# Two of five gate tiles added element by element with indirect DMAs, the other three by reworked one-hot products, in a decoder-trunk step

## The chip, the cores and the metric

The kernel runs as one launch on 1 core of a Trainium2 chip. The metric is the device time of one execution in microseconds (us). PE is TensorE, DVE is VectorE, ACT is ScalarE, POOL is GpSimd, and SP is the queue that issues the plain DMAs.

## The reference, cut to what matters

One step of a decoder layer for 1024 prompt tokens and 32 sample tokens, width 1024: attention and a gated recurrence, cross attention, then PEER, a layer of 16384 single-neuron experts. The change lies in PEER:

```python
def one_block(xc):
    q = (xc @ w_pq).reshape(blk, PEER_HEADS, PEER_QDIM)
    ...
    v1, i1 = lax.top_k(s1, PEER_TOPK)      # 16 of 128 first keys
    v2, i2 = lax.top_k(s2, PEER_TOPK)      # 16 of 128 second keys
    ...
    sc, ci = lax.top_k(cand, PEER_TOPK)    # 16 of the 256 pairs
    e = (jnp.take_along_axis(i1, ci // PEER_TOPK, axis=-1) * PEER_NKEYS
         + jnp.take_along_axis(i2, ci % PEER_TOPK, axis=-1))
    g = jax.nn.softmax(sc, axis=-1)
    u = peer_u[e]
    a = jax.nn.gelu(jnp.einsum('td,thkd->thk', xc, u))
    return jnp.einsum('thk,thkd->td', (g * a), peer_v[e])
```

Each token picks 8 x 16 = 128 experts, each with a gate g. The same expert may be picked by several heads of one token; its gates add up.

## The kernel before, in words

The tokens lie in nine tiles of 128 (tile 8 holds the 32 sample tokens), in three parts: tiles 0, 1, 2; then 3, 4, 8; then 5, 6, 7. Part by part each goes through `middle` (projections, attention, recurrence) and `tail` (cross attention, then `select`, which finds each token's experts and gates). Stages overlap: the middle of a part runs beside the tail of the part before (`run(W1, ...)`, `run(W2, ...)`), the last tail beside the late gates (`run(W3, ...)`). Which instruction comes when on each engine is set by a scheduler that plans with its own estimates of durations; on the chip each engine then works its list off in that order.

PEER is done in two ways. Tiles 0 to 4 (640 tokens) are dense: 128 iterations in `dense` run over all experts, 128 in each. An iteration loads a block of u and of v, makes the products `a` of the 640 tokens with u in two halves of 320 (48 matmuls), takes Gelu, multiplies by a 128 x 640 piece of the gate matrix (tile `gt`, from the DRAM tensor `gtall`), and multiplies with v. Tiles 5 to 8 are gathered: for each tile rows of u and then of v come by indirect DMA on POOL (line 1177, 832 in all, 512 KB each), and DVE makes the dot products (line 1184) and the weighted sums (line 1195). The gathers run beside the dense pass and begin before it.

The gate matrix of a dense tile is built in `gates(di)`. `select` leaves for each token its 128 first indices, second indices and gates, transposed, in `selD`. For every token a matrix with a 1 at (slot, first index), `hot[0]`, and one with the gate at (slot, second index), `hot[1]`, are multiplied on PE: the product over the slots is the token's 128 x 128 gates. In groups of four tokens: one DVE comparison of 512 elements for `hot[0]` (L1013); four DVE operations (L1018) for `hot[1]`, or, for two tokens of the four in tiles 2, 3 and 4, two ACT operations each (L1021, L1022); four matmuls (L1024), each into 128 neighbouring PSUM columns; a copy (L1027) that interleaves the tokens into staging tiles `sg`, `row`, `thi` or `tlo`; after 16 tokens a store to `gtall`. Tile 0, 1 and 2 are built beside part 2's middle, tiles 3 and 4 beside its tail.

POOL has little to do before the gathers: 25 small power operations (`rs_r`, L211) of the norms. The list of POOL is worked off in order, and so are SP's issues: one that waits holds all behind it.

Of the kernel before, what the change touches and what calls it, by code (L numbers as in the profile page):

```python
# [25 lines left out]
NG = sum(t in PARTS[0] for t in DENSE)  # L26
GT = 16
# [38 lines left out]
def _body(tc, nc, ctx, A, O):  # L66
# [22 lines left out]
    anchors = []  # L89

# [32 lines left out]
    DM_A, DM_X, SEL, BEX = misc[:, 0:8], misc[:, 8:12], misc[:, 12:28], misc[0:32, 28:36]  # L123
    iota16 = T(cst, [128, 16], BF16, "iota16")
# [174 lines left out]
    def part(pi):  # L299
# [624 lines left out]
    def select_tile(t, R, H, v, ix, scale):  # L924
# [47 lines left out]
        if t in DENSE:  # L972
            p = bank(SELB)
            for i in range(3):
                PE.transpose(out=p[:, i * 128 : (i + 1) * 128], in_=fnd[:, i], identity=ident)
            st = T(pk, [128, 4, 128], F32, "c2", 2)
            pv = p[:, :384].rearrange("p (i t) -> p i t", i=3)
            S.copy(st[:, 0:3], pv)
            S.activation(st[:, 3], pv[:, 2], AF.Copy, scale=-1.0)
            SP.dma_start(selD[DENSE.index(t)], st)  # L980
            return
        eu = T(pk, [128, 128], U32, "sc")[:R, :n]
        V.scalar_tensor_tensor(eu, fnd[:, 0], 128.0, fnd[:, 1], op0=ALU.mult, op1=ALU.add)
# [9 lines left out]
    def gates(di):  # L993
        st = T(wk, [128, 4, 128], F32, "x_vs")
        SP.dma_start(st, selD[di])
        late_ = di >= NG
        for blk in range(128 // GT):
# [10 lines left out]
            w = 128 // len(stg)  # L1008
            for q in range(GT // 4):
                p = bank(("g", "Ty", "Ts")[flip("gb", LB)] if late_ else "g")  # L1010
                t0 = blk * GT + 4 * q
                hot = [T(wk, [128, 4, 128], F32, "raw" if RAW else "oh", 2 if RAW else 3), T(wk, [128, 4, 128], F32, "oh", 3)]
                V.tensor_tensor(hot[0], iota.rearrange("p (o k) -> p o k", o=1).to_broadcast([128, 4, 128]),  # L1013
                                st[:, 0, t0 : t0 + 4].rearrange("p (t o) -> p t o", o=1)
                                .to_broadcast([128, 4, 128]), op=ALU.is_equal)
                for i in range(4):
                    if i >= LATE[di]:
                        V.tensor_scalar(hot[1][:, i], iota, col(st[:, 1], t0 + i), col(st[:, 2], t0 + i),  # L1018
                                        op0=ALU.is_equal, op1=ALU.mult)
                    else:  # L1020
                        S.activation(hot[1][:, i], iota, AF.Abs, bias=col(st[:, 1], t0 + i), scale=-1.0)  # L1021
                        S.activation(hot[1][:, i], hot[1][:, i], AF.Relu, bias=col(st[:, 2], t0 + i),  # L1022
                                     scale=col(st[:, 3], t0 + i))
                    PE.matmul(p[:, i * 128 : (i + 1) * 128], lhsT=hot[0][:, i], rhs=hot[1][:, i],  # L1024
                              start=True, stop=True)
                for i, sg in enumerate(stg):
                    ANY.tensor_copy(sg[:, :, 4 * q : 4 * q + 4].rearrange("p i t -> p t i"),  # L1027
                                    p.rearrange("p (t i) -> p t i", i=128)[:, :, i * w : (i + 1) * w])
            for i, sg in enumerate(stg):
                SP.dma_start(gtd[di * (128 // GT) + blk][:, i * w : (i + 1) * w], sg)  # L1030
            if blk % 2:
                yield

    def dense(dv, dn, dps):
# [14 lines left out]
        NH = M // GT // 2  # L1049

        def gate_piece(k, h, r):
            lo, hi = max(0, 8 * k - 4 * h), min(128, 8 * k - 4 * h + 8)
            if lo >= hi:
                return
            if r == 0:
                gts[k, h] = T(dn, [128, NH, 8, GT], F32, "gt", 3)
            n = NH // 4
            ins = SP.dma_start(gts[k, h][:, r * n : (r + 1) * n, : hi - lo].rearrange("p b i t -> p b (i t)"),
                         gtall[h * NH + r * n : h * NH + (r + 1) * n, :, lo * GT : hi * GT].rearrange("b p x -> p b x"))
            if k == 0:  # L1060
                after(ins, GA[0] - GA[1] * (4 * (1 - h) + r))

        def hidden(i, out):
            if i == 0:
                for h in (1, 0):
                    for r in range(4):
                        gate_piece(0, h, r)
            k, h = divmod(i // 4 + 2, 2)
            gate_piece(k, 1 - h, i % 4)
# [6 lines left out]
            for h in range(2):  # L1076
                lo, hi = h * (M // 2), (h + 1) * (M // 2)
                kg, ki = divmod(i + 4 * h, 8)
                ki -= 4 * h if kg == 0 else 0
                pa = T(dps, [128, 512], F32, "a", 6 - 2 * KEEP + 1 if KEEP > 2 else 2)[:, : M // 2]  # L1080
                mm3(pa, u, x, 8, slice(lo, hi))
                S.activation(ga[:, lo:hi], pa, AF.Gelu)  # L1082
                gv = ga[:, lo:hi].rearrange("p (b t) -> p b t", t=GT)
                V.tensor_tensor(gv, gv, gts[kg, h][:, :, ki], op=ALU.mult)  # L1084
# [155 lines left out]
    run(W0, p[0].middle(lambda: ahead(p[1])), memory_kv())  # L1240
# [123 lines left out]
```

## Time and profile before

| | |
|---|---|
| time, median of 3 runs | 3661.61 us (3661.39 to 3673.91) |
| the profiled execution: time, span | 3667.75 us, 3665.9 us |
| mean granted TensorE clock | 0.968 |
| busy share PE / DVE / ACT / POOL | 93% / 71% / 38% / 31% |
| mean DMA rate | 275 GB/s |

The profiled execution was 6.1 us longer than the median of the runs. Busy shares are means over stages: POOL is idle in the first two fifths of the span, and ACT is busier there than later.

### The profile page before, as it was taken

Reading aid. Unit: us, or ns where it says so; the run is one execution under the profiler, and the core shown is the slowest. Engines: PE = TensorE matmul, PEld = TensorE weight load, DVE = VectorE, ACT = ScalarE, POOL = GpSimd, SP = SyncE. Lnnn points to the kernel's source line nnn. Section 1 sums busy time; section 2 is a strip of 40 time slices with the busy share of each in tenths; the row PEclk is TensorE's granted clock in tenths of the full one; section 3 lists DMA queues with packets and bytes.
Section 4 is the critical chain, followed back from the end, with each engine's and each line's share of the span. In section 5 each row is a group of like instructions: output and inputs, shape, how many; then the busy total and the mean of one; then the engine's idle time right before and its main releaser. Section 6 shows DMA issues by size and latency. Waiting matters only on the chain.

```text
span 3665.9 us, 53269 instructions
## 1 busy us (share of the span) xinstructions
PE 3405.2 (93%) x19338; PEld 2936.3 (80%) x19338; DVE 2620.1 (71%) x6013; ACT 1400.8 (38%) x2674; POOL 1119.4 (31%) x871
## 2 busy tenths in 40 slices
PE   5999999999999789878699998999999999999996
PEld 4876776677987679778688987999988889988895
DVE  4444333243885776779988867998888888888897
ACT  4544344344435555786332222222222222222221
POOL 0000000000000000022236634665665555556564
PEclk9999999999999989989899999999999999999998
DMA  7667776656655476388879977999999899999897
GB/s 238 224 226 248 237 245 236 210 182 204 208 196 200 151 267 225 142 292 309 278 239 337 343 270 265 366 337 336 336 354 348 316 335 343 332 359 329 322 338 274
DMA packets 408518, 1007.86 MB, mean 275 GB/s; under 512 B 43968, under 2 KB 168896, under 8 KB 406848
## 3 DMA queue, kind: packets, MB, share of 16 engines
q1 hardware_dynamic: 288448, 568.20, 45.3%
q0 software_dynamic: 119808, 436.26, 32.6%
q8 instruction: 152, 2.49, 0.3%
q14 instruction: 110, 0.90, 0.1%
HBM read 866.01 MB, written 138.31 MB: 274 GB/s over the span
## 4 chain that ended last, share of the span: by engine, by line
PE 73%; DMA 8%; DVE 7%; issue 5%; ACT 5%; POOL 1%; SPq 0%; POOLq 0%; DVEq 0%; ACTq 0%
PE a L202 7%; PE a L204 7%; PE a L203 7%; PE y L1093 4%; PE y L1092 4%; PE y L1094 4%; PE z L202 4%; PE z L203 3%; PE z L204 3%; PE g L1024 3%; PE yr L1092 3%; PE y L202 2%; PE yr L1093 2%; PE yr L1094 2%; PE y L203 2%
## 5 line engine op out<-in xcount | busy, mean ns | idle before, releaser
L1177 POOL DMA_INDIRECT row<-in_peer_u,ix x416 | 541.9, 1303 | 585.9 <-DVE dots L1184 324.1
L1177 POOL DMA_INDIRECT row<-in_peer_v,ix x416 | 547.4, 1316 | 469.1 <-DVE ha L1195 331.6
L202 PE MATMUL a<-xh,u 128*128 128x320 f32 x2048 | 641.9, 313 | 41.9 <-ACT u L170 26.7
L204 PE MATMUL a<-xh,u 128*128 128x320 f32 x2048 | 638.3, 312 | 4.6 <-DVE u L171 4.6
L203 PE MATMUL a<-xl,u 128*128 128x320 f32 x2048 | 637.4, 311 | 0.0
L1195 DVE SCALAR_TENSOR_TENSOR ha<-row,dots,ha 128x1024 f32<-128x1024 f32 x416 | 533.1, 1282 | 10.6 <-DMA row<-in_peer_v,ix 7.0
L1184 DVE CUSTOM_DVE_ANT_0 row<-row,ha 128x1024 f32<-128x1024 f32 x416 | 497.6, 1220 | 50.5 <-DMA row<-in_peer_u,ix 50.2
L1082 ACT ACTIVATE w<-a 128x320 f32<-128x320 f32 x256 | 111.8, 437 | 909.4 <-PE a L204 906.3
L211 POOL TENSOR_TENSOR rs_r<-rs_m,mhalf 128x3 f32<-128x3 f32 (+2 forms) x25 | 21.3, 856 | 1384.3 <-DVE rs_m L209 1110.7
L202 PEld LDWEIGHTS a<-xh,u 128*128 128x128 f32 x2048 | 389.2, 190 | 65.6 <-ACT u L170 29.1
L203 PEld LDWEIGHTS a<-xl,u 128*128 128x128 f32 x2048 | 389.4, 190 | 8.3
L204 PEld LDWEIGHTS a<-xh,u 128*128 128x128 f32 x2048 | 388.8, 190 | 7.8 <-DVE u L171 6.3
L202 PE MATMUL z<-zhi,wz 128*128 128x384 f32 (+2 forms) x928 | 329.1, 355 | 34.7 <-ACT zhi L170 10.1
L203 PE MATMUL z<-zlo,wz 128*128 128x384 f32 (+2 forms) x928 | 316.2, 341 | 3.8 <-DVE zlo L171 2.1
L204 PE MATMUL z<-zhi,wz 128*128 128x384 f32 (+2 forms) x928 | 313.0, 337 | 0.0
L1092 PE MATMUL y<-v,w 128*128 128x512 f32 x768 | 297.5, 393 | 6.1 <-ACT w L170 6.1
L1093 PE MATMUL y<-v,w 128*128 128x512 f32 x768 | 301.0, 393 | 0.0
L1094 PE MATMUL y<-v,w 128*128 128x512 f32 x768 | 251.5, 390 | 1.6 <-DVE w L171 1.6
L202 PEld LDWEIGHTS z<-zhi,wz 128*128 128x128 f32 x928 | 180.3, 194 | 76.9 <-issue 19.0
L170 ACT CAST w<-w 128x320 fp32r<-128x320 f32 x256 | 117.7, 460 | 251.6 <-DVE w L1084 251.4
L1092 PE MATMUL yr<-v,w 128*128 128x512 f32 x512 | 203.3, 397 | 11.2 <-DVE ys L1121 9.6
L1093 PE MATMUL yr<-v,w 128*128 128x512 f32 x512 | 201.8, 394 | 0.0
(462 smaller groups left out, 6907.1 us busy)
## 6 DMA issues: line engine op xcount, KB each, us to landing
u<-in_uT SPq DMA_DIRECT2D x128, 512.0 KB, 7.0
v<-in_peer_v SPq DMA_DIRECT2D x128, 512.0 KB, 8.0
wz<-wd_w_in SPq DMA_DIRECT2D x112, 512.0 KB, 4.1
gt<-gtall SPq DMA_DIRECT2D x124, 320.0 KB, 12.0
wd_w_in<-wz SPq DMA_DIRECT2D x56, 512.0 KB, 3.2
gtall<-sg SPq DMA_DIRECT2D x34, 512.0 KB, 3.4
wd_w_pq<-wt SPq DMA_DIRECT2D x32, 512.0 KB, 2.9
wt<-wd_w_pq SPq DMA_DIRECT2D x32, 512.0 KB, 4.1
```

The lines of the kernel that those rows point to most:

```text
L170: S.copy(hi, src)
L202: PE.matmul(out, lhsT=whi, rhs=xhi[:, c, sl], start=c == 0, stop=False)
L203: PE.matmul(out, lhsT=whi, rhs=xlo[:, c, sl], start=False, stop=False)
L204: ins = PE.matmul(out, lhsT=wlo, rhs=xhi[:, c, sl], start=False, stop=c == kc - 1)
L1024: PE.matmul(p[:, i * 128 : (i + 1) * 128], lhsT=hot[0][:, i], rhs=hot[1][:, i], start=True, stop=True)
L1082: S.activation(ga[:, lo:hi], pa, AF.Gelu)
L1092: PE.matmul(o, lhsT=wh[:, sl], rhs=vh[:, ds], start=start and q == 0, stop=False)
L1093: PE.matmul(o, lhsT=wh[:, sl], rhs=vl[:, ds], start=False, stop=False)
L1094: PE.matmul(o, lhsT=wl[:, sl], rhs=vh[:, ds], start=False, stop=stop and q == len(ws) - 1)
L1177: G.indirect_dma_start(out=row, out_offset=None, in_=tab, in_offset=bass.IndirectOffsetOnAxis(ap=col(ix, j), axis=0))
L1184: V.tensor_tensor_reduce(row, row, hn, 1.0, 0.0, op0=ALU.mult, op1=ALU.add, accum_out=col(dots, j))
L1195: V.scalar_tensor_tensor(acc, row, col(dots, j), acc, op0=ALU.mult, op1=ALU.add)
```

## The change

- **Tiles 0 and 1** no longer go through `gates`. A DRAM tensor `gates` of 128 x 128 x 256 elements (16.8 MB) is cleared by 32 plain DMAs of 512 KB of zeros, issued by SP beside part 0's middle, each after a projection. `select` then writes for these tiles the place of each pick in this tensor, (second index x 128 + first index) x 256 + token, to `ixd`, and the gate to `gd`, in place of `selD`. `scatter` loads both and issues 128 indirect DMAs per tile on POOL (L1079), each of which adds 128 single elements (4 bytes) into `gates`.
- **Tiles 2, 3 and 4**: `select` splits the second index into quotient and remainder by 16. For 16 tokens, three small DVE operations make `high` (the gate at one of 8 places) and `low` (a 1 at one of 16); their product, one DVE operation of 512 elements for four tokens, is `hot[1]`. The ACT operations for it are gone. A matmul writes its 128 columns into every fourth PSUM element, and the copy reads PSUM in order and writes runs of four.
- **Dense**: an iteration loads a 128 x 256 piece of `gates` (tile `gs`, 128 KB, after the last scatter) and multiplies the first 256 tokens by it; the other 384 are multiplied by `gt`, now loaded for 24 blocks of 16 tokens in two buffers, where it was 20 in three. The halves are 256 and 384 tokens, where they were 320 and 320.

```diff
-        if t in DENSE:
+        if t in DENSE[NS:]:
+            qr = T(pk, [128, 3, 128], U16, "c2", 2)
...
+            V.tensor_scalar(qr[:, 1], qr[:, 0], 4, None, op0=ALU.logical_shift_right)
+            V.tensor_scalar(qr[:, 2], qr[:, 0], 15, None, op0=ALU.bitwise_and)
...
+        if t in DENSE:
+            V.scalar_tensor_tensor(fnd[:, 0], fnd[:, 1], 128.0, fnd[:, 0], op0=ALU.mult, op1=ALU.add)
+            V.tensor_scalar(eu, fnd[:, 0], float(NM), col(TOK, DENSE.index(t)), op0=ALU.mult, op1=ALU.add)
...
+            V.tensor_tensor(high, wide(st[:, 1, b0 : b0 + GT], GT, 8), steps(8), op=ALU.is_equal)
+            V.tensor_tensor(high, high, wide(st[:, 3, b0 : b0 + GT], GT, 8), op=ALU.mult)
+            V.tensor_tensor(low, wide(st[:, 2, b0 : b0 + GT], GT, 16), steps(16), op=ALU.is_equal)
...
                 for i in range(4):
-                    if i >= LATE[di]:
-                        V.tensor_scalar(hot[1][:, i], iota, col(st[:, 1], t0 + i), col(st[:, 2], t0 + i),
-                                        op0=ALU.is_equal, op1=ALU.mult)
-                    else:
-                        S.activation(hot[1][:, i], iota, AF.Abs, bias=col(st[:, 1], t0 + i), scale=-1.0)
-                        S.activation(hot[1][:, i], hot[1][:, i], AF.Relu, bias=col(st[:, 2], t0 + i),
-                                     scale=col(st[:, 3], t0 + i))
-                    PE.matmul(p[:, i * 128 : (i + 1) * 128], lhsT=hot[0][:, i], rhs=hot[1][:, i],
-                              start=True, stop=True)
+                    PE.matmul(p[:, :, i], lhsT=hot[0][:, i], rhs=hot[1][:, i], start=True, stop=True)
...
+    def clear_gates():
...
+        for n in range(128 * NM // 1024):
+            sync(SP.dma_start(rows[n], z.rearrange("p a b -> p (a b)")), prog[-1])
...
+                for j in range(16 * h, 16 * h + 16):
+                    ins = G.indirect_dma_start(out=gates_s, out_offset=bass.IndirectOffsetOnAxis(ap=col(ix, j), axis=0),
+                                               in_=col(gw, j), in_offset=None, compute_op=ALU.add)
...
+            gs = T(dn, [128, NM], F32, "gs", GTB)
+            ins = SP.dma_start(gs, gview[i])
+            for w_ in added:
+                sync(ins, w_)
...
-    run(W0, p[0].middle(lambda: ahead(p[1])), memory_kv())
+    run(W0, p[0].middle(lambda: ahead(p[1])), seq_of(memory_kv, clear_gates))
...
-    run(W1, p[1].middle(lambda: ahead(p[2])), seq_of(lambda: p[0].tail("T")), seq_of(sample_mix))
+    run(W1, p[1].middle(lambda: ahead(p[2])), seq_of(lambda: p[0].tail("T"), lambda: scatter(range(NS))), seq_of(sample_mix))
```

On POOL, before, six power operations stand between the tail of part 0 and the first gather (line 1177); what an instruction waits for is in brackets (DMAHW: a plain DMA, DMASW: one of POOL's own):

```order
L211 TENSOR_TENSOR rs_r_9424<-rs_m_9422,mhalf_100 128x3 [waits DVE_49,PE_49]
L211 TENSOR_TENSOR rs_r_10016<-rs_m_10014,mhalf_100 128x3 [waits DVE_49,PE_49,Pool_49]
L211 TENSOR_TENSOR rs_r_11019<-rs_m_11017,mhalf_100 128x3 [waits DVE_49,PE_49,Pool_49]
L211 TENSOR_TENSOR rs_r_11866<-rs_m_11864,mhalf_100 128x3 [waits DVE_49,PE_49,Pool_49]
L211 TENSOR_TENSOR rs_r_13384<-rs_m_13382,mhalf_100 128x3 [waits DVE_49,PE_49]
L211 TENSOR_TENSOR rs_r_13991<-rs_m_13989,mhalf_100 128x3 [waits DVE_49,PE_49,Pool_49]
L1177 DMA row_30085<-in_peer_u,ix_30075 128x1024 [waits DMAHW4_49,DMAHW5_49,DMAHW2_49,DMAHW6_49,DMAHW1_49,DMAHW7_49,DMAHW0_49,Activation_49]
```

After the change the same place of POOL's list begins with scatters of tile 0 (`gw_7710`), 13 of them alone, then tile 1's (`gw_7714`) in turn with them. The power operations stand among them (their lines are now L216); `rs_r_9693` is what `rs_r_9424` was:

```order
L216 TENSOR_TENSOR rs_r_9565<-rs_m_9563,mhalf_100 128x3 [waits DVE_49,PE_49]
L1079 DMA gates_163<-gw_7710,ix_7709 4194304x1 [waits DMAHW4_49,DMAHW5_49,DMAHW3_49,DMAHW6_49,DMAHW2_49,DMAHW7_49,DMAHW1_49,DMAHW0_49]
L1079 DMA gates_163<-gw_7710,ix_7709 4194304x1 [waits DMASW0_49]
L1079 DMA gates_163<-gw_7710,ix_7709 4194304x1 [waits DMASW1_49]
...
L1079 DMA gates_163<-gw_7710,ix_7709 4194304x1 [waits DMASW4_49]
L1079 DMA gates_163<-gw_7714,ix_7713 4194304x1 [waits DMASW5_49]
L1079 DMA gates_163<-gw_7710,ix_7709 4194304x1 [waits DMASW6_49]
L216 TENSOR_TENSOR rs_r_9693<-rs_m_9691,mhalf_100 128x3 [waits DVE_49,PE_49]
```

The eight DMASW semaphores go round, so each scatter waits for the one before it of its own tile: two chains of 128. The six power operations stand behind 25, 32, 69, 118, 118 and 195 of the scatters, and the first gather (L1243) behind 245, all 128 of tile 0's among them; the other 11 stand between gathers.

On SP, before, the loads for the first gathered tile (`gw`, `ix`) waited for plain DMAs only:

```order
L985 DMA gd_59_157<-c_2701_13357 128x32 [waits DMAHW2_49,DVE_49]
L1172 DMA gw_30076<-gd_59_157 128x32 [waits DMAHW2_49]
L984 DMA ixd_50_148<-sc_13378 128x32 [waits DVE_49]
L1030 DMA gtall_165<-thi_13434 128x2048 [waits DMAHW5_49,Activation_49]
L187 DMA wz_15298<-wd_w_pq_1_1405_6440 128x1024 [waits DMAHW6_49,PE_49]
L1171 DMA ix_30075<-ixd_50_148 128x32 [waits DMAHW7_49,DMAHW4_49]
```

After the change the load of `gw` reuses a buffer of tile 0's scatters and waits for their semaphores:

```order
L999 DMA gd_59_157<-c_2499_12582 128x32 [waits DMAHW1_49,DVE_49]
L1047 DMA gtall_164<-thi_12712 128x2048 [waits Activation_49]
L998 DMA ixd_50_148<-sc_12603 128x32 [waits DMAHW3_49,DVE_49]
L1238 DMA gw_29238<-gd_59_157 128x32 [waits DMASW5_49,DMASW6_49,DMASW4_49,DMASW7_49,DMASW3_49,DMAHW1_49,DMASW2_49,DMAHW4_49,DMASW1_49,DMASW0_49]
L1237 DMA ix_29237<-ixd_50_148 128x32 [waits DMAHW5_49,DMAHW3_49]
L192 DMA wz_13998<-wd_w_co_0_1350_6238 128x1024 [waits DMAHW6_49,PE_49]
L1047 DMA gtall_164<-tlo_13040 128x2048 [waits DMAHW7_49,Activation_49]
L192 DMA wz_14019<-wd_w_co_0_1355_6264 128x1024 [waits DMAHW0_49,PE_49]
```

Behind it stand the load of `ix`, five loads of weights for part 2's cross attention (`wd_w_co`), two of them shown, and the stores of later gates.

## Rows read from the trace of the kernel before

**Rows 1.** The page: busy time of each engine, share of the span, instructions.
```profile
PE 3405.2 (93%) x19338; PEld 2936.3 (80%) x19338; DVE 2620.1 (71%) x6013; ACT 1400.8 (38%) x2674; POOL 1119.4 (31%) x871
```

**Rows 2.** Busy time by stretch; clock, DMA share and GB/s stand last.
```profile
core 0: us, PE busy (x) PEld busy (x) DVE busy (x) ACT busy (x) POOL busy (x), PEclk, DMA share, GB/s
0.00:300.00 300.00, 245.42 (x1332) 207.67 (x1333) 128.03 (x361) 144.49 (x311) 4.97 (x9) 0.97 0.67 224
1066.00:1300.00 234.00, 210.02 (x1376) 171.90 (x1375) 163.52 (x541) 122.98 (x227) 4.38 (x5) 0.97 0.53 186
1300.00:1500.00 200.00, 179.97 (x1173) 167.54 (x1172) 149.17 (x636) 116.17 (x288) 0.97 (x1) 0.93 0.68 238
1500.00:1600.00 100.00, 79.45 (x521) 72.60 (x521) 67.38 (x191) 82.85 (x199) 10.44 (x8) 0.95 0.51 179
1600.00:1755.00 155.00, 125.85 (x769) 119.61 (x767) 137.91 (x527) 114.00 (x269) 31.30 (x31) 0.90 0.88 318
1755.00:1778.00 23.00, 1.65 (x6) 1.35 (x6) 22.03 (x137) 6.93 (x7) 0.35 (x2) 0.50 1.08 338
1778.00:3000.00 1222.00, 1186.95 (x6541) 1071.12 (x6542) 1034.49 (x1540) 327.27 (x521) 674.35 (x510) 0.98 0.89 317
3000.00:3400.00 400.00, 397.49 (x2219) 358.85 (x2218) 346.89 (x513) 105.90 (x174) 235.23 (x184) 1.00 0.94 342
```

**Rows 3.** Timeline of PE around the first matmul of the dense pass.
```profile
1755.31 1.65 PE L675 MATMUL m<-P,av 128*128 128x128 f32 x6 [2.83 <-ACT hq L678]
1778.07 0.63 PE L202 MATMUL a<-xh,u 128*128 128x320 f32 x1 [21.11 <-ACT u L170]
```

**Rows 4.** Instructions of lines 1013 and 1018 (min/median/max ns, first and last start).
```profile
L1013 DVE TENSOR_TENSOR raw<-iota,x_vs x160: 659/691/730, 1065.9 to 1730.5; 128x512 f32<-128x512 f32 x160
L1018 DVE TENSOR_SCALAR oh<-iota,x_vs x448: 325/341/350, 1066.5 to 1724.4; 128x128 f32<-128x128 f32 x150
```

**Rows 5.** Groups of ACT instructions by line and shape, 1000 to 1780 us.
```profile
L1022 ACT ACTIVATE oh<-oh,x_vs 128x128 f32<-128x128 f32 x192 | 84.7, 493 | 0.0
L1021 ACT ACTIVATE oh<-iota,x_vs 128x128 f32<-128x128 f32 x192 | 66.2, 399 | 58.7 <-PE g L1024 49.1 <-PE x L1024 4.4 <-DMA x_vs<-selD 3.4
...
L1027 ACT COPY sg<-g 128x256 f32<-128x256 f32 x105 | 62.8, 598 | 40.5 <-PE g L1024 39.5
...
L678 ACT COPY q<-x 128x256 f32<-128x256 f32 x15 | 5.9, 395 | 3.2 <-PE x L675 3.2
```

**Rows 6.** Busy time of line 1024's matmuls alone, sum over 1066 to 1755 us.
```profile
sum 689.00, PE 194.36 PEld 175.17; mean PE 48.59 PEld 43.79
```

**Rows 7.** Timeline of POOL; idle time before each instruction in brackets.
```profile
1106.60 0.97 POOL L211 TENSOR_TENSOR rs_r<-rs_m,mhalf 128x3 f32<-128x3 f32 x1 [81.56 <-PE o L469]
...
1476.12 0.97 POOL L211 TENSOR_TENSOR rs_r<-rs_m,mhalf 128x3 f32<-128x3 f32 x1 [178.73 <-DVE ggs L970]
1566.26 1.75 POOL L1177 DMA_INDIRECT row<-in_peer_u,ix  x1 [89.18 <-DMA wz<-wd_w_pq]
```

**Rows 8.** DMA issues: three row gathers (from 1625.89, 1629.22, 1635.01), us to landing.
```profile
row<-in_peer_u,ix POOLq DMA_INDIRECT x1, 4.1
...
row<-in_peer_u,ix POOLq DMA_INDIRECT x1, 4.8
...
row<-in_peer_u,ix POOLq DMA_INDIRECT x1, 5.7
```

**Rows 9.** DMA issues, 1556 to 1560 us, and of the whole run.
```profile
ixd<-sc SPq DMA_DIRECT2D x1, 16.0 KB, 1.4
...
wd_w_pq<-wt SPq DMA_DIRECT2D x32, 512.0 KB, 2.9
```

**Rows 10.** Timeline of POOL: a gather that waited for nothing shown.
```profile
1589.86 0.94 POOL L1177 DMA_INDIRECT row<-in_peer_u,ix  x1 [0.30 <-issue]
```

**Rows 11.** Timeline of SP's DMA issues.
```profile
1556.21 0.32 SPq L1172 DMA_DIRECT2D gw<-gd  x1
```

More of the change, by code (lines that the diff above doesn't have):

```diff
@@ L36 @@
 GA = (10, 1)
+GTB = 4
 EARLY = 90
@@ new lines, in gates @@
+                sl = slice(4 * q, 4 * q + 4)
+                V.tensor_tensor(hot[1].rearrange("p t (a b) -> p t a b", b=16),
+                                high[:, sl].rearrange("p t (a o) -> p t a o", o=1).to_broadcast([128, 4, 8, 16]),
+                                low[:, sl].rearrange("p t (o b) -> p t o b", o=1).to_broadcast([128, 4, 8, 16]),
+                                op=ALU.mult)
+                for i in range(4):
+                    PE.matmul(p[:, :, i], lhsT=hot[0][:, i], rhs=hot[1][:, i], start=True, stop=True)
@@ L1031, in gates, with sync @@
             if blk % 2:
                 yield
+    def clear_gates():
+        z = T(pk, [128, 8, 128], F32, "tw", 2)
+        V.memset(z, 0.0)
+        rows = gates_s.rearrange("(n p x) o -> n p (x o)", p=128, x=1024)
+        for n in range(128 * NM // 1024):
+            sync(SP.dma_start(rows[n], z.rearrange("p a b -> p (a b)")), prog[-1])
+            if n % 4 == 3:
+                yield
+    added = []
+    def sync(ins, to):
+        tc.add_manual_dep(ins.ins, to.ins.name,
+                          mybir.DependencyInfo(mybir.DependencyClass.Sync, mybir.DependencyReason.DATA), reason="gates")
@@ new lines, in scatter @@
+    def scatter(dis):
+        ins_ = {}
+        for di in dis:
+            ix = T(gat, [128, 128], U32, "ix", 2)
+            gw = T(gat, [128, 128], F32, "gw", 2)
+            SP.dma_start(ix, ixd[DENSE[di]])
+            SP.dma_start(gw, gd[DENSE[di]])
+            ins_[di] = (ix, gw, [])
+        for h in range(8):
+            for di in dis:
+                ix, gw, last = ins_[di]
+                made = []
+                for j in range(16 * h, 16 * h + 16):
+                    ins = G.indirect_dma_start(out=gates_s, out_offset=bass.IndirectOffsetOnAxis(ap=col(ix, j), axis=0),
+                                               in_=col(gw, j), in_offset=None, compute_op=ALU.add)
+                    for d in range(NS):
+                        for k in range(8):
+                            if d != di or k == h:
+                                tc.declare_no_dep(ins.ins, group=f"gates{d}_{k}", reason="no two of these write one element")
+                    for w_ in last:
+                        sync(ins, w_)
+                    made.append(ins)
+                for ins in made:
+                    tc.add_to_no_dep_group(f"gates{di}_{h}", ins.ins)
+                last[:] = made
+            yield
+        for di in dis:
+            added.extend(ins_[di][2])
@@ L1239, in _body @@
     p[0].first_h()
[L1240 removed]
+    run(W0, p[0].middle(lambda: ahead(p[1])), seq_of(memory_kv, clear_gates))
     p[1].first_h()
[L1242 removed]
+    run(W1, p[1].middle(lambda: ahead(p[2])), seq_of(lambda: p[0].tail("T"), lambda: scatter(range(NS))), seq_of(sample_mix))
     p[2].first_h()
[L1244 removed]
+    run(W2, p[2].middle(), seq_of(lambda: p[1].tail("T")), seq_of(*[lambda i=i: gates(i) for i in range(NS, NG)]))
     run(W3, p[2].tail("Z"), seq_of(*[lambda i=i: gates(i) for i in range(NG, len(DENSE))]))
```

90 lines of the change are left out of this document (51 added, 39 removed).

## The prediction

> **What bounds the kernel now.** I read the page first: PE is busy 93% of the span, POOL 31% [rows 1]. A mean says little here, so I cut the span where the change works. From 1066 us, when the first comparison for tile 0's gates runs [rows 4], to 1778 us, when the first matmul of the dense pass starts [rows 3], PE is busy for 597 of 712 us, DVE for 540 and ACT for 443 (sums of five stretches), and the DMA share is between 0.53 and 0.68 until 1600 us [rows 2]. No engine is full; they hand work to each other, with PE nearest. The last 178 us of it differ: from 1600 to 1755 us DVE has 138 of 155, and from 1755 to 1778 us it has 22 of 23 while PE waits 21 us for the first block of u [rows 2, 3]. In the dense pass PE is the bound: 397.5 of 400 us between 3000 and 3400, with 35 us idle between 1778 and 3000 [rows 2]. So what the change can earn is an earlier start of the dense pass. On POOL the front is nearly empty: six power operations of under 1 us from 1107 to 1476 us, then the first gather at 1566 us [rows 7].
>
> **What is removed.** Two of five tiles leave the one-hot products. PE loses two fifths of 194 us [rows 6]: **78 us**. DVE loses 64 comparisons of 0.69 us and 256 operations of 0.34 us [rows 4]: 44 + 87 = 131 us. ACT loses 128 copies at 0.60 us, 77 us, and for tiles 2 to 4 the 192 pairs, 85 + 66 = 151 us [rows 5].
>
> **What is added to the one-hot products of tiles 2 to 4.** 96 products of 512 elements at 0.69 us (66 us) take the place of 192 operations at 0.34 (65 us). `high` and `low` cost, for 24 blocks of 16 tokens, two operations of 128 elements and one of 256; between 0.34 for 128 and 0.69 for 512 that is 0.34 + 0.34 + 0.45, 27 us in all. DVE's net is -104 us. The copies now write runs of four; an ACT copy of 128 x 256 in plain order takes 0.40 us, the interleaving one 0.60 [rows 5], so they lose between nothing and 0.2 us each, on an engine that is not the bound. The matmuls write every fourth PSUM element. No row of before shows such a write: between no cost, which I take as all else of the instruction stays, and twice the time, which would give 3/5 of 194 us, 117 us, back to PE.
>
> **How far the front could shrink.** With nothing new in the way, I take PE's term: 1066 to 1778 would be 78 us shorter. DVE's 104 us is the upper bound; below, if only part of PE's work lay on the path, 40.
>
> **The clears.** 16.8 MB in the first 300 us, where DMA has a share of 0.67 at 224 GB/s [rows 2]; at 224/0.67 = 334 GB/s they are 50 us of all engines, beside 99 us that are free, while PE is idle for 55 of the 300 us. All hidden gives 0, all exposed 50; most of the free time is spread out, so I take a quarter, 12 us.
>
> **The scatters.** This is the new term. Each waits for the one before of its tile, so a tile's chain lasts 128 steps, and only the step counts: POOL's instruction, the transfer, the landing, the wake-up. Before has no such DMA. The nearest rows are single row gathers of 512 KB, 4.1, 4.8 and 5.7 us from issue to landing, POOL's instruction (0.94 us in [rows 10]) included [rows 8]. A 512 KB store takes 2.9 us and a 16 KB store 1.4 [rows 9], so 1.5 us of a gather are its bytes. POOL wakes about 0.3 us after what it waits for; I take that from the wait before gathers called issue, 0.30 each [rows 10]. That gives 2.9, 3.6 and 4.5 us. Bounds from farther rows: the 16 KB store with 1 us of POOL in place of SP's 0.3 and the wake-up, 1.4 + 0.7 + 0.3 = 2.4; a whole slow gather, 5.7 + 0.3 = 6.0. I take **3.6**, the row in the middle: the DMA share is lower beside the scatters than beside those gathers (0.53 to 0.68 against 0.88 [rows 2]), but an addition must first read what is there, which is in none of these rows. Two chains alternate on POOL at about 1 us an instruction, so POOL itself allows 2 us a step and does not bind.
>
> The Trainium skill ("DMA: Bandwidth & Descriptors", section "Anatomy of one DMA — SWDGE (gpsimd) path") gives a fixed 2.0 us for such a DMA and next to nothing for so few bytes; by an estimate from that figure and the wake-up the step would be near 2.3 us, or 3.3 with POOL's instruction on top, and the chain would hide. The row of the 4.1 us gather, less its bytes, lies 0.6 us over that figure before the wake-up, so the traces here do not quite bear it out.
>
> **Who waits for the chain.** On SP the load of `gw` for the first gathered tile waits for tile 0's last scatter, and behind it on SP wait `ix`, weights of part 2's cross attention and gate stores. On POOL the first gather stands behind 245 scatters, and the power operations of part 2 and the last tails behind 25 to 195. So when the chain is late, the last tail is late. Before, the issue of `gw` at 1556.2 led to the first gather at 1566.3 [rows 7, 11], 10 us; and from the first gather to the dense pass 212 us passed [rows 3, 7]. That last stretch loses little: its DVE work is mostly selection and the dot products, and it keeps gates of tiles 3 and 4, whose DVE work grows by `high` and `low`. I keep 212.
>
> **The sum.** Dense start = 1066 + 12 + 128 x 3.6 (461) + 10 + 212 = **1761 us**, against 1778: -17. Without the chain it would be 1778 - 78 + 12 = 1712, so the chain sets the end. The dense pass itself: halves of 256 and 384 columns are as many columns as 2 x 320, so PE's 48 + 30 matmuls per iteration stay; the gate bytes stay; ACT's and DVE's operations stay in number. One more load per iteration is on SP. PE's 35 us idle there is what could be got by larger pieces per row; between 0 and 35 I take a quarter, 9 us. In all -26 us. The profiled execution took 3667.75 us with a span of 3665.9 (the table), 6.1 over the median; it would become 3642, and on the scale of the median 3661.6 - 26 = **3635 us**.
>
> **Rivals.**
> 1. The chain is late (slower). Its place is the wait of `gw` and the power operations in POOL's list; the price is 128 us for each us of step. 1066 + 12 + 128 L + 10 + 212 equals 1778 at L = 3.73; with the 9 us of the dense pass the kernel is no faster from L = 3.81, and slower by 18 us from 3.95. At 4.5, the slowest of the three gathers, it is 3750. For it: gathers that meet other traffic land in 5.7 and more, and a step adds to what it first has to read. Against it: small transfers and the two faster gathers.
> 2. The chain hides (more gain). From L = 3.2 down the front's own 66 us (78 - 12) count: 3661.6 - 66 - 9 = 3587; with DVE's 104 in place of 78, 3561. For it: the 16 KB store's bound of 2.4. The Trainium skill's figure above points the same way.
> 3. PSUM writes in steps are slow. At twice the time PE gets 117 us back, more than the 78 it lost; as PE is busy in 84% of the front and the chain leaves it idle besides, I take the front at 1778 + 12 + (117 - 78) = 1829 at worst, 1790 if half hides: 3665 to 3704. The Trainium skill ("PSUM — Partial Sum Buffer", section "Specifications (TRN2)") warns of just this: any non-contiguous pattern slows matmuls significantly. No row of before shows it either way.
> 4. The clears are exposed by 50 in place of 12: dense at 1799, time 3674, no change.
> 5. The change earns nothing since the last stretch is DVE's: then only the dense pass's 9 us are left, 3653, no change.
>
> **How the numbers follow.** Forecast 0.36 (steps between 3.2 and 3.8: 3587 to 3660), chain hidden 0.26, chain late 0.20, PSUM 0.08, clears or nothing 0.10. Faster by over 0.5% (18 us, about what a measurement of this kernel can tell from no change): 0.26 of the forecast, 0.26, and 0.02 of the others, 0.54. Within it: 0.10 of the forecast, 0.02 of the late chain, 0.03 and 0.06: 0.21. Slower: 0.18 + 0.05 + 0.02: 0.25. The range leaves out the longest chains (a step over 4.3 is 3661.6 + 128 x 0.49 = 3724) and gains beyond DVE's 104: **3560 to 3725**. The forecast's own range is 3587 to 3660.
>
> **What would show it.** Right: scatters of one tile some 3.6 us apart on POOL, each ended by a DMA to `gates`; tile 0's last near 1540 us, the first gather near 1550, the first `a` matmul near 1760; matmuls of the gates as long as before; SP idle at the load of `gw` for part of the stretch before 1540. Wrong in the step: another distance, and the dense start moved by 128 times the difference. Wrong in the mechanism: power operations no later than their DVE inputs, and PE waiting elsewhere. Wrong in PSUM: gate matmuls over 0.4 us. Wrong in the clears: PE more than 12 us longer up to 300 us. Wrong in the dense pass: PE idle growing at waits for `gs` or `gt`.

## The result and the profile after

The changed kernel takes **3750.4 us** (median of 4 runs, 3740.9 to 3761.2) against 3661.5 us before: a ratio of 1.025, 95% interval [1.021, 1.028]. It is slower, by 89 us; the prediction was 3635, in a range that ended at 3725. The profiled execution has a span of 3744.5 us.

Busy time by stretch of the changed kernel, the columns as in [rows 2] (POOL's is the fifth pair, then the clock, DMA share and GB/s):

```profile
0.00:300.00 300.00, 242.17 (x1328) 207.15 (x1329) 127.10 (x360) 147.34 (x313) 4.84 (x9) 0.98 0.75 265
1066.00:1300.00 234.00, 172.62 (x1053) 134.29 (x1052) 117.34 (x341) 80.82 (x173) 144.05 (x91) 0.88 0.58 147
1300.00:1500.00 200.00, 140.25 (x891) 130.18 (x892) 83.47 (x424) 38.52 (x95) 132.13 (x87) 0.83 0.70 184
1500.00:1600.00 100.00, 52.29 (x260) 45.05 (x261) 57.98 (x209) 31.74 (x69) 80.15 (x48) 0.72 0.37 63
1600.00:1755.00 155.00, 91.55 (x602) 85.61 (x601) 95.69 (x183) 39.80 (x85) 86.49 (x57) 0.80 0.70 219
```

Up to 300 us PE is as busy as before (242 against 245 us) although DMA's share rose from 0.67 to 0.75: the clears are there and hold nothing up. From 1066 us POOL, nearly empty before, is busy for 144 of 234 us, and PE is less busy than before in each stretch (some of its work is gone) and has a lower granted clock (0.83 where it was 0.93 from 1300 to 1500 us). The scatters, with min/median/max of the instruction in ns and first and last start, and their time from issue to landing, counted from the start of POOL's instruction:

```profile
L1079 POOL DMA_INDIRECT gates<-gw,ix x256: 1532/1542/3967, 1056.9 to 1738.9; - x128
...
DMA to landing us min/median/max: 2.8/3.5/10.4
```

The landing, 3.5 us in the median, is about what the row gathers had suggested. POOL's instruction is not: 1.54 us, where the quickest row gathers took 0.94 [rows 10]. The median one of the kernel before took 1.24:

```profile
L1177 POOL DMA_INDIRECT row<-in_peer_u,ix x416: 935/1242/3224, 1566.3 to 3344.9; - x139
```

Five places of POOL's timeline (idle time before each instruction and its releaser in brackets):

```profile
1056.87 1.74 POOL L1079 DMA_INDIRECT gates<-gw,ix  x1 [46.02 <-issue]
1061.86 1.61 POOL L1079 DMA_INDIRECT gates<-gw,ix  x1 [3.25 <-DMA gates<-gw,ix]
...
1250.62 1.54 POOL L1079 DMA_INDIRECT gates<-gw,ix  x1 [0.30 <-issue]
1252.47 1.54 POOL L1079 DMA_INDIRECT gates<-gw,ix  x1 [0.30 <-issue]
1253.46 1.47 POOL L216 TENSOR_TENSOR rs_r<-rs_m,mhalf 128x3 f32<-128x3 f32 x1
...
1542.48 1.46 POOL L216 TENSOR_TENSOR rs_r<-rs_m,mhalf 128x3 f32<-128x3 f32 x1
...
1645.66 1.54 POOL L1079 DMA_INDIRECT gates<-gw,ix  x1 [0.30 <-issue]
...
1652.69 1.01 POOL L1243 DMA_INDIRECT row<-in_peer_u,ix  x1 [0.30 <-issue]
```

While tile 0's chain runs alone, the first 13 scatters start 4.8 us apart in the mean, and each waits some 2 to 4 us for the one before. Their landings are slower than the median of all (DMA issues, 1057 to 1114 us, median us to landing last):

```profile
gates<-gw,ix POOLq DMA_INDIRECT x12, 4.7
```

Once two chains alternate, most follow each other after 1.54 + 0.30 us with nothing to wait for but POOL, and such a pair takes 3.7 us; 79 of the 230 up to tile 0's last still wait for a landing, 110 us in all. Tile 0's last starts at 1645.7 us, 589 us after its first; **a step is 4.6 us**. The power operations stand in the list: the one that ran at 1230.8 us before [rows 7] starts at 1253.5, the one of 1476.1 at 1542.5. PE waits for some of them (us in total, times, longest):

```profile
PE x L223 <- POOL rs_r L216: 38.0, 1, 38.0
PE x L573 <- POOL rs_r L216: 28.8, 1, 28.8
PE h L223 <- POOL rs_r L216: 19.9, 2, 14.2
```

On SP the load of `gw` is issued when tile 0's chain has ended; `ixd`, ahead of it in the queue, was stored 48 us earlier:

```profile
1601.06 0.32 SPq L998 DMA_DIRECT2D ixd<-sc  x1
1648.68 0.32 SPq L1238 DMA_DIRECT2D gw<-gd  x1
```

The first gather starts at 1652.7 us (1566.3 before) and the first matmul of the dense pass, with its last behind it in this row, 99 us later than before:

```profile
L207 PE MATMUL a<-xh,u x2048: 274/333/687, 1877.4 to 3689.9; 128*128 128x256 f32 x94, 128*128 128x384 f32 x93
```

From there to the end of the span it takes 1867 us, 21 less than before.

### The profile page after: what moved, and what is told of

It is laid out like the page before. It is cut to its first block, busy times and chain, and to the rows that moved or that the text cites. A ratio compares the mean times of both kernels' runs of the same rounds, so it can differ in the third digit from the quotient of the medians.

```text
span 3744.5 us, 51682 instructions
## 1 busy us (share of the span) xinstructions
PE 3334.9 (89%) x18823; PEld 2874.2 (77%) x18823; DVE 2549.4 (68%) x5693; ACT 1176.3 (31%) x2152; POOL 1521.6 (41%) x1127
## 4 chain that ended last, share of the span: by engine, by line
PE 65%; DMA 16%; POOL 7%; issue 6%; DVE 4%; ACT 2%; SPq 0%; POOLq 0%; ACTq 0%; DVEq 0%
DMA gates<-gw,ix 9%; PE a L207 7%; PE a L209 7%; PE a L208 7%; POOL gates L1079 5%; PE y L1158 4%; PE y L1159 4%; PE y L1160 4%; PE yr L1159 3%; PE yr L1158 3%; PE yr L1160 3%; PE z L207 3%; PE z L208 2%; PE z L209 2%; PE s L409 2%
## 5 line engine op out<-in xcount | busy, mean ns | idle before, releaser
L1243 POOL DMA_INDIRECT row<-in_peer_u,ix x416 | 536.4, 1290 | 508.2 <-DVE dots L1250 314.8
L1243 POOL DMA_INDIRECT row<-in_peer_v,ix x416 | 537.5, 1292 | 421.4 <-DVE ha L1261 293.4
L207 PE MATMUL a<-xh,u 128*128 128x256 f32 (+1 forms) x2048 | 637.0, 311 | 17.7 <-ACT w L1145 17.5
L209 PE MATMUL a<-xh,u 128*128 128x256 f32 (+1 forms) x2048 | 634.6, 310 | 0.0
L208 PE MATMUL a<-xl,u 128*128 128x256 f32 (+1 forms) x2048 | 634.0, 310 | 0.0
L1079 POOL DMA_INDIRECT gates<-gw,ix x256 | 417.3, 1630 | 264.4 <-DMA gates<-gw,ix 169.5
L1145 ACT ACTIVATE w<-a 128x256 f32<-128x256 f32 (+1 forms) x256 | 112.0, 438 | 999.7 <-PE a L209 988.1
L216 POOL TENSOR_TENSOR rs_r<-rs_m,mhalf 128x3 f32<-128x3 f32 (+2 forms) x25 | 24.5, 1009 | 945.0 <-DVE rs_m L214 775.3
L207 PE MATMUL z<-zhi,wz 128*128 128x384 f32 (+2 forms) x928 | 334.7, 361 | 57.2 <-DMA wz<-wd_w_pq 24.2
L209 PE MATMUL z<-zhi,wz 128*128 128x384 f32 (+2 forms) x928 | 319.0, 344 | 0.0
L1158 PE MATMUL yr<-v,w 128*128 128x512 f32 x512 | 200.9, 392 | 8.2 <-DVE ys L1187 4.2
L207 PE MATMUL y<-thi,wt 128*128 128x288 f32 (+2 forms) x576 | 191.1, 332 | 13.7 <-DMA wt<-wd_w_pq 10.0
```

What stands on the lines that cost most here:

```text
L207: PE.matmul(out, lhsT=whi, rhs=xhi[:, c, sl], start=c == 0, stop=False)
L208: PE.matmul(out, lhsT=whi, rhs=xlo[:, c, sl], start=False, stop=False)
L209: ins = PE.matmul(out, lhsT=wlo, rhs=xhi[:, c, sl], start=False, stop=c == kc - 1)
L1079: ins = G.indirect_dma_start(out=gates_s, out_offset=bass.IndirectOffsetOnAxis(ap=col(ix, j), axis=0), in_=col(gw, j), in_offset=None, com ...
L1158: PE.matmul(o, lhsT=wh[:, sl], rhs=vh[:, ds], start=start and q == 0, stop=False)
L1243: G.indirect_dma_start(out=row, out_offset=None, in_=tab, in_offset=bass.IndirectOffsetOnAxis(ap=col(ix, j), axis=0))
```

## The experiments

Times are medians; ratios are to the kernel before, with 95% intervals.

**1. No scatters.**

```diff
-                for j in range(16 * h, 16 * h + 16):
+                for j in range(0):
```

> All of the change but the 256 scatters: the clears stay, nothing is added, so the gates of tiles 0 and 1 are zero. Theory A (the scatters alone cost the time: they hold POOL's list and the load of gw): the front becomes shorter than before, by the 78 us of PE's term less little for the clears, and the dense pass gives the 21 us that the changed kernel's trace shows; 3661 - 78 - 21, so 3550 to 3590 us, and the first matmul of the dense pass near 1700 us. Theory B (the last stretch, from the first gather to the dense pass, and the clears cost it too): the dense pass starts at 1760 or later, 3640 us or more.

Measured: 3586.8 us, 0.976 [0.972, 0.981]. The power operations and the first gather on POOL, and the start of the dense pass on PE:

```profile
1205.01 0.85 POOL L216 TENSOR_TENSOR rs_r<-rs_m,mhalf 128x3 f32<-128x3 f32 x1 [85.45 <-DVE rs_m L214]
1275.15 1.67 POOL L216 TENSOR_TENSOR rs_r<-rs_m,mhalf 128x3 f32<-128x3 f32 x2 [69.29 <-DVE rs_m L214]
1428.44 0.87 POOL L216 TENSOR_TENSOR rs_r<-rs_m,mhalf 128x3 f32<-128x3 f32 x1 [151.62 <-DVE rs_m L214]
1488.42 1.16 POOL L1243 DMA_INDIRECT row<-in_peer_u,ix  x1 [59.11 <-DMA ix<-ixd]
```

```profile
L207 PE MATMUL a<-xh,u x2048: 274/333/691, 1708.6 to 3532.2; 128*128 128x256 f32 x94, 128*128 128x384 f32 x93
```

Theory A holds, with 1708.6 us for the dense pass. All the rest of the change together, with the gates of two tiles left out, is worth 75 us, and the scatters cost 164. Their cost shows in the start of the dense pass: 1877.4 - 1708.6 = 169 us.

**2. The chain cut to groups of 16.** Each scatter joins its group before the next is made, so that no dependency is drawn between two of one head:

```diff
                     made.append(ins)
-                for ins in made:
                     tc.add_to_no_dep_group(f"gates{di}_{h}", ins.ins)
```

> Scatters of one head of a tile wait no longer for one another, only each group of 16 for the group before. In POOL's list four of the power operations of part 2 now stand behind all 256. Theory A (the step is latency: 3.5 us of landing; POOL's own instruction is about 1 us and would hide): 256 scatters take 256 x 1.24 = 317 us, the four power operations come near 1375 us, and the kernel is at 3650 to 3800 us. Theory B (the step is POOL's own 1.54 us instruction and 0.30 us between two, and two chains in turn already hide most of the latency): 256 x 1.85 = 474 us, the power operation that came at 1253 us comes at 1530 or later, and the kernel is slower than the changed one, by 100 us or more: 3850 to 4030 us.

Measured: 3865.4 us, 1.054 [1.048, 1.060]. The scatters (and the idle time ahead of them that a DMA ended), and POOL's timeline at their end:

```profile
L1079 POOL DMA_INDIRECT gates<-gw,ix x256: 1539/1551/2484, 1065.3 to 1552.5; - x128
...
  DMA gates<-gw,ix: 2.6, 1
```

```profile
1552.50 1.55 POOL L1079 DMA_INDIRECT gates<-gw,ix  x1 [0.30 <-issue]
1553.51 3.10 POOL L216 TENSOR_TENSOR rs_r<-rs_m,mhalf 128x3 f32<-128x3 f32 x3
1711.75 0.88 POOL L216 TENSOR_TENSOR rs_r<-rs_m,mhalf 128x3 f32<-128x3 f32 x1 [155.14 <-DVE rs_m L214]
1770.05 1.41 POOL L1242 DMA_INDIRECT row<-in_peer_u,ix  x1 [57.42 <-DMA ix<-ixd]
```

Theory B. The landings are waited for 2.6 us in all, and 256 scatters still take from 1065 to 1554 us, 1.9 us each. Three power operations run at once behind them all, the first of them 348 us late (1205.0 without scatters), and PE, DVE and the gathers with them. The scatters are done sooner (1.9 us each, where it was 2.4), but the edit let the scheduler move the power operations: the third now stands behind all 256 scatters, where it stood behind 69. So this run does not show what the waits for landings cost by themselves; experiment 6 keeps the order.

**3. Buffers of their own for the scatters' `ix` and `gw`.**

```diff
-            ix = T(gat, [128, 128], U32, "ix", 2)
-            gw = T(gat, [128, 128], F32, "gw", 2)
+            ix = T(gat, [128, 128], U32, "ixs", 2)
+            gw = T(gat, [128, 128], F32, "gws", 2)
```

> The scatters' ix and gw get buffers of their own, so that on SP the load of gw for the first gathered tile waits for no scatter; POOL's list is the same. Theory A (POOL's list sets the delay: the first gather and six power operations stand behind scatters): no change against the changed kernel, 3735 to 3765 us, first gather still near 1650 us. Theory B (SP's wait of 47 us, with weights and gate stores behind it, sets it): 3700 to 3710 us.

Measured: 3767.7 us, 1.027 [1.021, 1.032]. SP issues `gw` as soon as its data is there:

```profile
1611.78 0.32 SPq L1238 DMA_DIRECT2D gw<-gd  x1
```

The first gather still comes at 1670.1 us, released by nothing but POOL's list, and the dense pass starts at 1889.9:

```profile
1670.08 1.01 POOL L1243 DMA_INDIRECT row<-in_peer_u,ix  x1 [0.30 <-issue]
```

Theory A, 3 us above its range (3753 to 3777 us, the changed kernel 3741 to 3761): SP's wait was real but not the one that ended last.

**4. Half of the scatters.**

```diff
-                for j in range(16 * h, 16 * h + 16):
+                for j in range(16 * h, 16 * h + 8):
```

> Every head's picks 8 to 15 are left out, so 64 scatters for a tile, 128 in all; chained as in the changed kernel. At the 2.4 us per scatter of the changed kernel they end near 1365 us, 120 us before the first gather is due, and SP's load of gw waits no more. Theory B1 (only the late first gather costs): within 15 us of the kernel without scatters, 3575 to 3600 us. Theory B2 (the power operations among the first 118 scatters cost as well; in the changed kernel PE waits 38 + 29 + 20 us for them): 25 to 60 us more, 3612 to 3645 us.

Measured: 3666.7 us, 1.002 [1.000, 1.003]. POOL from the last scatter to the first gather:

```profile
1421.40 1.54 POOL L1079 DMA_INDIRECT gates<-gw,ix  x1 [5.41 <-DMA gates<-gw,ix]
1511.88 1.30 POOL L216 TENSOR_TENSOR rs_r<-rs_m,mhalf 128x3 f32<-128x3 f32 x1 [88.93 <-DVE rs_m L214]
1572.26 1.12 POOL L1243 DMA_INDIRECT row<-in_peer_u,ix  x1 [59.08 <-DMA ix<-ixd]
```

The chains end at 1421 us, 67 us before the first gather of the kernel without scatters, and yet this one's is at 1572.3. It is 84 us late because the power operation ahead of it is 84 us late (1511.9 against 1428.4); it in turn waited for DVE work behind the earlier ones, at 1255.8 in place of 1205.0 and 1358.7 in place of 1275.2. This is theory B2, with a larger sum (80 us) than its 25 to 60: one power operation hands its delay to the next, and it grows, 51, 84 and 84 us for these three.

**5. Plain writes in place of additions.**

```diff
-                    in_=col(gw, j), in_offset=None, compute_op=ALU.add)
+                    in_=col(gw, j), in_offset=None)
```

> The scatters write the gate and do not add it (where two heads pick one expert, only one gate is left); chain and list are unchanged. Theory D (the addition makes POOL's instruction 1.54 us where a row gather's shortest is 0.94): the instruction takes about 1 us, a pair of scatters 2.6 in place of 3.7 where no landing is waited for, and the kernel is 60 us or more faster than the changed one: under 3690 us. Theory E (128 single elements cost POOL that much, added or not): 1.5 us again and 3735 to 3765 us.

Measured: 3659.9 us, 1.000 [0.998, 1.002].

```profile
L1079 POOL DMA_INDIRECT gates<-gw,ix x256: 952/958/3358, 1059.1 to 1640.0; - x128
...
DMA to landing us min/median/max: 2.1/3.3/9.2
```

Theory D: the instruction takes 0.96 us. The landing hardly changes (3.3 us against 3.5). The 0.58 us that adding costs POOL, on 245 scatters ahead of the first gather, are worth 90 us of the kernel's time. The first scatter and tile 0's last, the 243rd on POOL:

```profile
1059.14 1.18 POOL L1079 DMA_INDIRECT gates<-gw,ix  x1 [46.27 <-issue]
...
1551.48 0.96 POOL L1079 DMA_INDIRECT gates<-gw,ix  x1 [0.30 <-issue]
```

That is 3.9 us a step in place of 4.6. So with POOL at the 1 us that the prediction took, the step is still longer than its 3.6, and the kernel is no faster than before. 90 us for 0.76 us of step is 119 us for each us; the prediction said 128.

**6. A chosen order.** The chain cut as in 2, buffers as in 3, every scatter tied to the power operation that it follows, and tile 1's scatters behind tile 0's, no longer in turn; `UPTO` says how many scatters stand ahead of each power operation.

```diff
+    UPTO = (0, 0, 0, 24, 30, 82, 114, 114, 200, 256)
...
+    def before_pow():
+        if todo:
+            pump(UPTO[min(len(pows), len(UPTO) - 1)])
```

> All 256 scatters, chained by groups of 16 only, with buffers of their own, and in POOL's list the power operations stand behind 24, 30, 82, 114, 114 and 200 scatters: at 1.88 us each that is when the kernel without scatters runs them (1109 to 1428 us). All 256 stand before the first gather. Theory B (POOL's list, at 1.85 to 1.9 us a scatter, is all that they cost): the power operations are on time, the first gather comes near 1057 + 256 x 1.88 = 1540 us, some 50 us after that of the kernel without scatters (1488), and the kernel is at 3625 to 3650 us. Theory C (the additions also cost through their DMA traffic or the loads of the dense pass): over 3670 us.

> As the paced kernel, but the last 40 scatters stand behind 15 or so of the first gathers. Theory B: 216 x 1.88 = 406 us end at 1465, before the first gather of the kernel without scatters (1488); 40 x 1.9 = 76 us of POOL lie beside the first gathers, which wait for DVE most of the time. The kernel comes within 20 us of the one without scatters (3587): 3580 to 3605 us, faster than the kernel before and than the one-hot rework alone (3632). Theory C: over 3640 us.

Measured: 3695.5 us, 1.009 [1.006, 1.012], and split (216 in place of 256, the rest emitted with the dense pass) 3689.7 us, 1.008 [1.006, 1.011]. By the numbers that is theory C in both. The trace gives another account; the split one on POOL:

```profile
1483.94 1.46 POOL L217 TENSOR_TENSOR rs_r<-rs_m,mhalf 128x3 f32<-128x3 f32 x1
...
1544.84 2.80 POOL L1260 DMA_INDIRECT row<-in_peer_u,ix  x1 [22.18 <-ACT sg L1046]
```

The operation due at 1428.4 us runs at 1483.9. My 1.88 us per scatter left out the waits between groups, 44 us in all, so the operations were late again, by 28 us at the third (1232.9) and 56 at the last. The first gather is 56 us late by that, and the dense pass starts 258 us after it (1803.0) where it was 220 without scatters; 40 scatters lie beside the gathers there. 56 + 38 = 94 of the 103 us over experiment 1. The 56 are theory B's. The 38 were not separated by a run, but the trace points to POOL's list: between gathers the scatters stand in blocks of 8, 16 and 16, DVE waits 14 us for a gathered row behind the second block, and the DMA share of the stretch is lower than without scatters (0.83 against 0.92). Without the split, no scatter stands beside the gathers, and the stretch takes 220 us (1606.6 to 1826.2). Nor do the additions slow the dense pass: from its start to the end of the span it takes 1870 us, split 1884, and 1881 without scatters.

Against the changed kernel, whose power operations stand behind nearly the same numbers of scatters, the unsplit one is 55 us faster. What it does away with is most of POOL's waits for landings (44 us in all, where the changed kernel has 170); own buffers gained nothing in experiment 3. That points to landings for about a third of the 164 us, and to POOL's own time for the rest.

**7. The one-hot rework alone**, for all five tiles, without scatters; and the same with the columns of PSUM as before:

```diff
-                    PE.matmul(p[:, :, i], lhsT=hot[0][:, i], rhs=hot[1][:, i], start=True, stop=True)
+                    PE.matmul(p[:, i * 128 : (i + 1) * 128], lhsT=hot[0][:, i], rhs=hot[1][:, i], start=True, stop=True)
...
-                    ANY.tensor_copy(sg[:, :, 4 * q : 4 * q + 4], p[:, i * w : (i + 1) * w])
+                    ANY.tensor_copy(sg[:, :, 4 * q : 4 * q + 4].rearrange("p i t -> p t i"),
+                                    p.rearrange("p (t i) -> p t i", i=128)[:, :, i * w : (i + 1) * w])
```

> The reworked one-hot products with PSUM written in steps, for all five tiles, and nothing of the scatters, clears or dense halves. Sum by rows: ACT loses 151 us of one-hot operations and 0.22 us on each of some 280 copies of 256 columns, DVE is level (153 us of small comparisons against 110 of products and 45 of high and low), PE is level. Theory A (PE's waits for these copies and one-hots, 17 + 13 + 8 us and some smaller ones, were on the path): 3615 to 3640 us. Theory B (they were cover, the front is set by other things): 3650 to 3665 us. Theory C (PSUM in steps costs PE): over 3680 us.

> The one-hot rework alone, but each matmul writes 128 neighbouring PSUM columns and the copy interleaves the tokens again, as in the kernel before; the products of high and low stay. Theory F (the gain of the rework, 30 us, comes from the quicker copies, 0.37 in place of 0.60 us, for which PE waited): 3650 to 3665 us. Theory G (it comes from ACT's one-hot operations that are gone): 3625 to 3640 us, the same as the rework with steps. Theory H (PSUM in steps costs PE something that the copies hide): faster than the rework, under 3625 us.

Measured: 3632.2 us, 0.991 [0.987, 0.995], and with plain columns 3648.6 us, 0.996 [0.994, 0.998]. PE's waits for the copies with steps, and then without:

```profile
PE g L1032 <- ACT sg L1034: 11.1, 12, 1.8
PE g L1032 <- ACT row L1034: 6.4, 10, 1.5
```

```profile
PE g L1032 <- ACT sg L1034: 16.9, 16, 2.2
PE g L1032 <- ACT row L1034: 12.6, 14, 1.6
```

Theory A of the first. The second lies between the ranges of F and G, just below F's: of some 30 us, 16 come with the quicker copies, and 13 with the rest of the rework, ACT's one-hot operations that are gone among it. The rework alone brings the dense pass forward by 35 us (1778.1 before):

```profile
L201 PE MATMUL a<-xh,u x2048: 303/309/636, 1743.3 to 3565.9; 128*128 128x320 f32 x187
```

**8. One tile scattered**, with the order of 6, and then with dense halves of 320 columns again.

```diff
-NS = 2
+NS = 1
...
-    UPTO = (0, 0, 0, 24, 30, 82, 114, 114, 200, 256)
+    UPTO = (0, 0, 0, 12, 12, 44, 70, 70, 116, 128)
```

> Only tile 0 by scatters (128, chained by groups of 16, own buffers), tiles 1 to 4 by the reworked products, halves of 128 and 512; the power operations stand behind 12, 12, 44, 70, 70 and 116 scatters, all 128 before the first gather. Theory B (what counts is how late POOL's list runs the power operations): 12, 44, 70 and 116 scatters at 1.88 us end at 1080, 1140, 1190 and 1275 us, each before the operation is due, so they cost nothing, the saving is that of one tile less of products, half of the way from the one-hot rework alone (3632) to the kernel without scatters (3587): 3600 to 3620 us. Theory C (scatters cost something besides, in step with their number, as 100 us for 256 in the paced kernels): 3650 to 3665 us.

Measured: 3760.5 us, 1.025 [1.020, 1.030]. Neither theory; the halves of 128 and 512 columns, which came with the edit, were a change of their own. PE in the dense pass, 512 columns and then 128:

```profile
2403.48 0.39 PE L207 MATMUL a<-xh,u 128*128 128x512 f32 x1
2403.70 0.39 PE L208 MATMUL a<-xl,u 128*128 128x512 f32 x1
...
2406.14 0.27 PE L209 MATMUL a<-xh,u 128*128 128x128 f32 x1
2406.25 0.28 PE L207 MATMUL a<-xh,u 128*128 128x128 f32 x1
```

> As the kernel with one tile scattered, but the dense halves are 320 and 320 columns again (the first half takes its gates from both tensors). In that kernel a 128-column matmul of the dense pass came every 0.112 us and a 512-column one every 0.2275, 24 of each 8.15 us, where 48 of 320 columns at 0.147 take 7.06: 1.09 us in each of 128 iterations, 140 us. Its front was as theory B said: power operations at 1106, 1122, 1211, 1277 and 1445 us, first gather at 1496, dense pass from 1733. Theory B: 3760 - 140 = 3605 to 3630 us. Theory C (scatters cost something besides): over 3650 us.

Measured: **3602.6 us, 0.984 [0.981, 0.986]**: faster than both kernels, and the fastest here that leaves no work out. POOL's last power operation ahead of the gathers and the first gather:

```profile
1447.74 0.95 POOL L217 TENSOR_TENSOR rs_r<-rs_m,mhalf 128x3 f32<-128x3 f32 x1 [58.61 <-DVE rs_m L214]
1499.49 1.49 POOL L1258 DMA_INDIRECT row<-in_peer_u,ix  x1 [27.28 <-ACT thi L1046]
```

Theory B, a little better than its range. With 128 scatters the last operation is 19 us and the first gather 11 us later than without scatters. At 256 the same kind of order had cost 103 us, so the cost is not in step with the number; these traces show it as a matter of room in POOL's list. No run has one tile left out without scatters; half way between 3632 and 3587 would be 3609 us.

## Why the prediction was wrong

Rival 1 came true: it gave 3750 us for a step of 4.5 us, and 4.6 us and 3750.4 us were measured. That the time fits so well is in part luck. The rival argued with landings as slow as the slowest gather's, and most of the step's excess was POOL's own time. With 4.6 us its sum would be 1066 + 12 + 589 + 10 + 212 = 1889, and 3764 us; the chain began 21 us earlier than it has it, the last stretch took 13 us longer, and the dense pass gained 21 us and not 9. The likeliest case had the right place and the wrong size.

- **The step that failed** is the size of the scatters' step, 3.6 us taken and 4.6 measured, so 589 us for the chain where the sum has 461; and in it, above all, "Two chains alternate on POOL at about 1 us an instruction, so POOL itself allows 2 us a step and does not bind". POOL takes 1.54 us for an addition and 0.30 between two, 3.7 us a pair; the remaining 0.9 us of the 4.6 are waits for landings, 4.8 us a step while one chain is alone, and the power operations among them. With plain writes of 0.96 us the step is 3.9 (experiment 5), so of the 1.0 us that the forecast lacked, 0.76 is what adding costs POOL. The other 0.3 is landings taken too short: while a chain had POOL to itself, a step took 4.8 us, and 4.0 with plain writes. The 0.94 us for POOL was the quickest row gather's; the median of before was 1.24.
- **A second path stood beside the sum's.** I let the chain act through its end alone, 1066 + 12 + 461 + 10 + 212. The prediction named the power operations as waiting but gave them no price. Without scatters the last of them ahead of the gathers runs at 1428, in the changed kernel at 1542. That alone makes 114 of the 164 us by which the first gather is late (1652.7 against 1488.4): the store of `ixd`, which this gather needs, is issued at 1601. The other 50 are scatters that still stand ahead of the gather, so here the end of the chain comes last, as the sum had it. Experiment 4 shows the first path alone.
- **The front without the chain**: forecast 1712 us for the start of the dense pass, measured 1708.6, but by luck. The sum took all of it from the two tiles that leave PE (78 us) and nothing from the rework of the other three. The rework alone brings 35 us (experiment 7), and taking the two tiles out as well brings 35 more.
- **The clears**: 12 us taken. The power operation of 1106.6 us came at 1109.1 without scatters and at 1102.9 in experiment 7, which has no clears; the next came at 1117.3 and 1118.3. So it is 6 us at most, and it does not last.
- **PSUM in steps**: right at no cost. The matmul is 275 ns in the median before and after, eight in a row take 1.14 to 1.16 us in both kernels of experiment 7, and the copy of 256 columns is 0.37 us where it was 0.60 [rows 5]. The matmuls before, and then matmuls and copies after:

```profile
L1024 PE MATMUL g<-oh,raw x944: 270/275/582, 1130.0 to 1735.2; 128*128 128x128 f32 x189
```

```profile
L1043 PE MATMUL g<-oh,raw x432: 270/275/582, 1179.2 to 1784.5; 128*128 128x128 f32 x144
```

```profile
L1045 ACT COPY sg<-g x54: 365/373/403, 1202.4 to 1785.2; 128x256 f32<-128x256 f32 x54
```

  The Trainium skill ("PSUM — Partial Sum Buffer", section "Specifications (TRN2)") says that a non-contiguous pattern slows matmuls significantly. These fp32 matmuls into every fourth element do not show it, so the measurement decides.
- **From the first gather to the dense pass**: 212 us kept, 225 measured, and 220 without scatters. **The dense pass**: 9 us of gain taken, 21 measured. But the same pass gains only 7 us without scatters (1881 us from its start to the end of the span), so the larger pieces per row are at most part of it.
- **A reading**: the DMA share from 1500 to 1600 us is 0.51 [rows 2], so "between 0.53 and 0.68 until 1600 us" starts a little too high; nothing rests on it.
- **The Trainium skill's figure for the transfer** ("DMA: Bandwidth & Descriptors", section "Anatomy of one DMA — SWDGE (gpsimd) path"): 2.0 us fixed. The shortest landings here are 2.1 us without the addition and 2.8 with it, the medians 3.3 and 3.5; it is a lower end, and it gives no figure for POOL's 1.54 us, which decided.

Left open: why adding costs POOL 0.58 us, how much of PE's time in the late front is its lower clock, and why the dense pass takes between 1867 and 1884 us in the kernels with halves of 256 and 384.

## What to carry to other kernels

Count a chain of small DMAs by the issuing engine's own time as well as by its landing, and measure that time for the very form: an addition cost 1.6 times a plain write. Then look at what else stands in that engine's list: short operations on the critical path, queued behind 25 to 195 slow ones, delay the kernel even where the chain itself ends early (80 us in experiment 4), and cutting the chain's dependencies let the scheduler put all 256 ahead of some of them (experiment 2). Before giving up on such a change, do half of it: one tile instead of two, in a chosen order, fits between the operations and turns 2.5% slower into 1.6% faster, of which the reworked products alone are worth 0.9%.

## What the hardware showed that was not expected

- 128 single elements of 4 bytes added by one indirect DMA: 1.54 us of POOL, written plainly 0.96 us; landing 3.5 and 3.3 us in the median. A chain of such additions that has POOL to itself took 4.8 us a step.
- A matmul of the dense pass with 128 columns was issued every 0.11 us, one with 512 every 0.23 (experiment 8; the granted clock was 1.00 there, its upper level): a quarter of the columns takes half of the time. The kernel with halves of 128 and 512 took 158 us longer than that with 320 and 320; the 256 and 384 of the change cost nothing that shows.
